# Second half's sum of squares from rows of x, memory's factors behind the first query pair, and no split of x on GpSimd, in the opening of a one-layer hybrid decoder kernel

## The chip, the cores and the metric

One core of one Trainium2 chip runs the kernel. Its five engines are TensorE (PE, with its weight loads as PEld), VectorE (DVE), ScalarE (ACT), GpSimd (POOL) and SyncE (SP, which issues nearly all transfers here). Each takes its own list of instructions in order, and semaphores join them. The metric is the device time of one execution in microseconds; the median of three runs of the kernel before is 894.69 us.

## The reference

One layer over 1024 rows of width 1024, with four cross-attention heads over a memory of 256 rows, four GLA heads and four HGRN2 heads, then a final norm. What the change touches is the head of it:

```python
h = x * rsqrt(mean(x * x, -1) + 1e-6) * norm_w            # 1024 rows
proj = h @ w_in                                           # queries, keys, values, gates of all groups
m = mem * rsqrt(mean(mem * mem, -1) + 1e-6) * mem_norm_w  # 256 rows
mk, mv = split(m @ w_mem_kv)
p = softmax(split_heads(xq) @ mk.T * 128 ** -0.5)         # then p @ mv, norms, silu(gate), w_out
```

## The kernel before

**Tiles.** x comes transposed (`xT`): eight column tiles (128 columns of x by 512 rows) for the first half of the rows, `x[0][k]` (tiles `A_96` to `A_103`), and eight for the second, `x[1][k]` (`A_104` to `A_111`). In products, float32 operands are split in a high part (a cast on ACT, L176 for x, L1269 for weights) and a low part (a subtraction, L177 for x, L1270 for weights), and three matmuls (L1500, L1501, L1502) stand for one product of two tiles.

**Products.** Projections use block sums of x. `A12` and `A11` are the first half's tiles 4 to 7 and 0 to 3, `A22` the second half's tiles 4 to 7, `S1` the second half's tiles 0 to 3 plus 4 to 7, and `S2`, `S3`, `S4` further sums and differences of both halves (`more_sums`). The first query pair `q0` (two heads, `pair_direct`) uses A12, A11, S1 and A22, 24 matmuls each. The gate pair of the first group follows (`pair`): A11, S1, S2, A12, S3, S4, A22, 12 matmuls each. Then cross-attention starts with scores (`sc`).

**Norm.** `norm_x(h)` squares the eight column tiles of a half on ACT (L1366, L1369) and adds them up on DVE (L1370). `norm_x_factors` sums over partitions with four matmuls (L224) and forms the factors (L212 to L217: logarithm and exponential on ACT, one Newton step on DVE). `norm_spread` puts them on a diagonal (L232) and spreads them by a matmul with ones (L233). `norm_scale` scales the tiles on DVE (L1382). `first_half` then splits A12, its low parts on POOL, and A11 on DVE. `second_half` forms S1 and A22; the low parts of A22 alternate between POOL and DVE.

**Memory.** `memory` gives the products for the keys (`key`, L1463), those for the values (`val`, L1474, 16 matmuls in four parts, accumulated in the banks `o` and `kv`), `scales` (the memory rows' factors by the same L224, L212 to L217, L232, L233) and `finish` (keys scaled and split).

**Order.** `run` emits the units in the order of its text. The tile framework then puts each engine's list in an order of its own by data dependences and a model of durations, so that places in the lists move further than the source says. SP takes its transfers in order with eight in flight: each waits for the landing of the one eight places ahead. Weight tiles come by `prefetch` into five buffers `wst`, their parts lie in five buffers each, `whi` and `wlo`.

Of the kernel before, what the change touches and what calls it, by code (L numbers as in the profile page):

```python
# [13 lines left out]
AF = mybir.ActivationFunctionType  # L14
ALU = mybir.AluOpType
AX = mybir.AxisListType
PSUM = bass.MemoryType.PSUM

P = 128
# [5 lines left out]
HALF = S // 2  # L25
# [1193 lines left out]
class Fast(Trunk):  # L1219
# [141 lines left out]
    def norm_x(self, h):  # L1361
# [8 lines left out]
                nc.vector.tensor_tensor(sm, sm, sq, op=ALU.add)  # L1370
        self.sm = sm

    def halves(self, name, x, eng):
        hi, lo = self.a_tile(), self.a_tile()
        self.split((hi, lo), x, eng)
        self.A.setdefault(name, []).append((hi, lo))
# [13 lines left out]
    def first_half(self):  # L1390

        nc = self.nc
        self.A = {}
        self.norm_spread()
        self.norm_scale(0, range(4, 8))
        for k in range(4, 8):
            self.halves("A12", self.x[0][k], nc.gpsimd)
        self.norm_scale(0, range(4))
        for k in range(4):
            self.halves("A11", self.x[0][k], nc.vector)  # L1400

    def second_half(self):

        nc = self.nc
        x, y = self.x
        self.norm_spread()
        self.norm_scale(1, range(4, 8))
        self.norm_scale(1, range(4))
        for k in range(4):
            t = self.t("h", [P, HALF], bufs=2)  # L1410
            nc.vector.tensor_tensor(t, y[k], y[k + 4], op=ALU.add)
            self.halves("S1", t, nc.vector)
            self.halves("A22", y[k + 4], nc.vector if k % 2 else nc.gpsimd)
            nc.vector.tensor_tensor(y[k + 4], t, x[k], op=ALU.subtract)

    def more_sums(self):
# [14 lines left out]
    def memory(self):  # L1431


        nc = self.nc
        mm = nc.tensor.matmul
        scaled = [self.t("mh", [P, 2, M], bufs=4) for _ in range(4)]
        x_ = lambda k: self.memT[k // 4][:, k % 4]
        xs = lambda k: scaled[k // 2][:, k % 2]
        sm = self.t("acc", [P, M], bufs=3)
        rb = self.t("o", [P, M], bufs=self.o_bufs)  # L1440
        col = self.c("col", [P, 8])
        for k in range(KT):
            nc.vector.tensor_scalar(xs(k), x_(k), self.vec[:, V_MNW + k : V_MNW + k + 1], None, op0=ALU.mult)
        for k in range(KT):
            if k == 0:
                nc.scalar.square(sm, x_(k))
            else:
                sq = self.t("h", [P, M], bufs=2)
                nc.scalar.square(sq, x_(k))
                nc.vector.tensor_tensor(sm, sm, sq, op=ALU.add)  # L1450

        self.mk = self.t("v", [P, 2, 4, M], F32R, bufs=1)
        self.mv = self.t("aux", [P, 2, HALF], bufs=1)
        accs, held = [], []

        def key(i):
            def f():
                if i % 2 == 0:
                    held.append(self.ps("tr" if i else "oT", [P, 2, M]))
                ps = held[i // 2][:, i % 2]  # L1460
                for k in range(KT):
                    w = self.mw["mk", i, k // 4][:, (k % 4) * P : (k % 4 + 1) * P]
                    mm(ps, w, xs(k), start=k == 0, stop=k == KT - 1)  # L1463

            return f

        def val(i):
            def f():
                if not accs:
                    accs.extend([self.ps(t, [P, HALF]) for t in ("o", "kv")])  # L1470
                for j in range(2):
                    k = 2 * i + j
                    for b in range(2):
                        mm(accs[b], xs(k)[:, b * P : (b + 1) * P], self.mw["mv", i, j], start=k == 0, stop=k == KT - 1)  # L1474
                if i == 3:
                    for b in range(2):
                        nc.scalar.activation(self.mv[:, b], accs[b], AF.Copy, scale=col[:, b : b + 1])

            return f

        def scales():
            ps = self.ps("sc", [P, M])
            self.factors(sm, col, 2)
            self.spread(ps, col, 2)
            nc.scalar.activation(rb, ps, AF.Copy, scale=QSCALE)

        def finish(j):
            def f():
                t = self.t("h", [P, M], bufs=2)
                nc.vector.tensor_tensor(t, held[j // 2][:, j % 2], rb, op=ALU.mult)  # L1490
                self.split((self.mk[:, 0, j], self.mk[:, 1, j]), t, nc.vector)

            return f

        return [key(i) for i in range(4)], [val(i) for i in range(4)], scales, [finish(j) for j in range(4)]


# [603 lines left out]
    def run(self):  # L2101
        nc = self.nc
        self.scm_i = 0
        self.sums = {}
        groups = [{"kind": kind, "n": n} for kind, n in GROUPS]
        groups[-1]["last"] = True
        first, fill = [], []
        x0, x1 = groups[:2]
        q0 = self.xq_units(x0, 0, self.pair_direct)
        first.append(self.gate_units(x0))  # L2110
        fill.append(self.xq_units(x1, 1) + self.gate_units(x1))
        first.append([])
        for i, g in enumerate(groups):
            if i >= 1:
                if i >= 2:
                    n, kind = g["n"], g["kind"]
                    if kind == "G":
                        u = self.glr_units() if n == 0 else []
                        u += self.gates_gla(g, n) + self.v_units(g, GV + 256 * n)
                        u += self.gate_units(g) + self.qk_units(g, n)  # L2120
                    else:
                        u = self.hf_units(g, n) + self.v_units(g, HI + 256 * n)
                        u += self.gate_units(g) + self.hq_units(g, n)
                    first.append(u)
                fill.append(self.out_units(groups[i - 1], False))
        last = self.out_units(groups[-1], True)

        self.setup()
        key, val, scales, finish = self.memory()
        self.load_x(0, range(8))  # L2130
        self.mw_mv("mv", 0, 1)
        self.load_x(1, range(8))
        self.mw_mv("mv", 2, 3)
        self.prefetch()
        for f in key:
            f()
        self.norm_x(0)
        self.norm_x_factors()
        val[0]()
        self.first_half()  # L2140
        val[1]()
        scales()
        self.norm_x(1)
        self.norm_x_factors()
        val[2]()
        val[3]()
        self.second_half()
        for n, f in enumerate(q0):
            f()
            if n == 7:  # L2150
                self.more_sums()
        for f in finish:
            f()
        for i, g in enumerate(groups):
            self.emit(g, first[i])
            while self.bg or i != 1 and self.tail:
                self.background()
            self.loop(g, fill[i])
        for i, f in enumerate(last):
            f()  # L2160
            if self.tail and (i == 0 or i >= 6):
                self.tail.pop(0)()
        assert self.gcol == NFLAG and self.n_prep == len(self.ops), (self.gcol, self.n_prep, len(self.ops))
# [79 lines left out]
```

## Time and profile before

| | |
|---|---|
| median of 3 runs | 894.69 us (894.6 to 895.03) |
| the profiled execution | 894.56 us, its span 892.8 us |
| PE busy | 856.5 us (96%) |
| DVE, ACT, POOL busy | 626.2, 529.6, 92.5 us |
| PE waits from 20 to 60, 60 to 80, 80 to 100, 100 to 130 us | 4.7, 3.7, 1.9, 0 us |
| granted clock of PE, 43 to 49 us | 0.50 |

The profile's times run from the start of the span; the execution's own time is 1.76 us longer than the span. An engine's row in a timeline has the start, the busy time of the row (several instructions where it ends in x2 and so on), what was done, and in brackets how long the engine sat idle before it and what it waited for. Matmuls overlap, so the pitch of their starts is what one costs. For DVE and ACT too, the pitch is a little below the duration. [...]

### The profile page before, as it was taken

To read this page: it belongs to the slowest core of one execution; us is meant where nothing else is said; L and a number is where in the kernel's file an instruction comes from. 1 tells how busy PE (TensorE), PEld (TensorE's weight loads), DVE (VectorE), ACT (ScalarE), POOL (GpSimd) and SP (SyncE) were. 2 spreads that over 40 slices of the span, in tenths; PEclk is the share of its full clock that TensorE was granted. 3 is DMA by queue.
4 is the path that set the end of the run, shared out by engine and by line. 5 is a ranking of instruction groups with operands and counts; after the bars stand their busy time and mean duration, and the time that the engine had idled before them with its cause. 6 is when DMAs were issued, how large, how long until landed. Compare 5 with 4: busy or idle time off the path is not lost.

```text
span 892.8 us, 13855 instructions
## 1 busy us (share of the span) xinstructions
PE 856.5 (96%) x4742; PEld 714.4 (80%) x4742; DVE 626.2 (70%) x1504; ACT 529.6 (59%) x1273; POOL 92.5 (10%) x111
## 2 busy tenths in 40 slices
PE   8788999999999999999999999999999999999994
PEld 7466887788888898888888898878977878877873
DVE  5879663657648885788648875787685777666676
ACT  4536967987435764467436754466963358942374
POOL 0212112321000110011000110011000011000012
PEclk9989999999999999999999999999999999999997
DMA  9410222451225612472235511473113561034764
GB/s 321 163 48 0 62 69 63 162 199 41 78 84 189 213 49 66 134 236 87 79 107 189 190 60 59 153 229 103 48 48 122 176 208 38 25 110 135 265 220 183
DMA packets 61120, 111.84 MB, mean 125 GB/s; under 512 B 6960, under 2 KB 7088, under 8 KB 61040
## 3 DMA queue, kind: packets, MB, share of 16 engines
q1 hardware_dynamic: 60752, 110.59, 37.4%
q8 instruction: 39, 0.64, 0.3%
q14 instruction: 41, 0.34, 0.1%
q10 hardware_dynamic: 288, 0.28, 0.1%
HBM read 77.28 MB, written 33.55 MB: 124 GB/s over the span
## 4 chain that ended last, share of the span: by engine, by line
PE 69%; DVE 13%; DMA 7%; ACT 7%; issue 3%; SPq 0%; POOL 0%; DVEq 0%; POOLq 0%; ACTq 0%
PE pp L1502 16%; PE pp L1500 16%; PE pp L1501 16%; DMA acc<-sum 3%; DVE acc L1997 2%; PE sc L1500 1%; PE o L1500 1%; DVE A L177 1%; PE sc L1502 1%; DMA A<-w_dram 1%; PE sc L1501 1%; DMA A<-xT_dram 1%; PE oT L982 1%; PE o L1501 1%; PE o L1502 1%
## 5 line engine op out<-in xcount | busy, mean ns | idle before, releaser
L1269 ACT CAST whi<-wst 128x512 fp32r<-128x512 f32 x193 | 117.5, 619 | 181.2 <-PE pp L1501 125.5
L1500 PE MATMUL pp<-A,whi 128*128 128x512 f32 x508 | 203.5, 402 | 3.1 <-ACT A L176 1.5
L1501 PE MATMUL pp<-A,whi 128*128 128x512 f32 x508 | 202.0, 398 | 2.2 <-DVE A L177 2.2
L1502 PE MATMUL pp<-A,wlo 128*128 128x512 f32 x508 | 201.9, 398 | 1.5 <-DVE wlo L1270 1.4
L1270 DVE TENSOR_TENSOR wlo<-wst,whi 128x512 fp32r<-128x512 f32 x193 | 131.7, 689 | 80.9 <-ACT whi L1269 76.3
L1500 PEld LDWEIGHTS pp<-A,whi 128*128 128x128 f32 x508 | 95.8, 189 | 27.5 <-ACT A L176 2.7
L1502 PEld LDWEIGHTS pp<-A,wlo 128*128 128x128 f32 x508 | 95.7, 188 | 26.4 <-DVE wlo L1270 3.6
L1501 PEld LDWEIGHTS pp<-A,whi 128*128 128x128 f32 x508 | 96.0, 189 | 25.6 <-DVE A L177 3.5
L1500 PE MATMUL pp<-whi,mh 128*128 128x512 f32 (+1 forms) x258 | 104.7, 406 | 0.3 <-DVE acc L1997 0.3
L1501 PE MATMUL pp<-wlo,mh 128*128 128x512 f32 (+1 forms) x258 | 102.7, 398 | 0.0
L1502 PE MATMUL pp<-whi,ml 128*128 128x512 f32 (+1 forms) x258 | 101.9, 395 | 0.6 <-POOL ml L992 0.6
L1997 DVE TENSOR_TENSOR acc<-acc,pp 128x512 f32<-128x512 f32 x112 | 76.6, 685 | 31.9 <-PE pp L1502 14.5
L992 POOL TENSOR_TENSOR ml<-h,mh 128x512 fp32r<-128x512 f32 x30 | 41.1, 1369 | 334.4 <-ACT mh L990 334.3
L1262 DVE TENSOR_TENSOR wst<-wst 128x512 f32<-128x512 f32 x82 | 56.9, 694 | 1.5
L1502 PEld LDWEIGHTS pp<-whi,ml 128*128 128x128 f32 x258 | 48.7, 189 | 10.4 <-POOL ml L992 1.0
L1501 PEld LDWEIGHTS pp<-wlo,mh 128*128 128x128 f32 x258 | 48.8, 189 | 7.8 <-DVE wlo L1270 0.3
L1500 PEld LDWEIGHTS pp<-whi,mh 128*128 128x128 f32 x258 | 48.7, 189 | 7.9 <-DVE acc L1997 0.5
L177 POOL TENSOR_TENSOR qk<-qk 128x128 fp32r<-128x128 f32 x28 | 13.0, 470 | 292.8 <-ACT qk L176 253.6
L1955 ACT ACTIVATE o<-o,rs_r 128x128 f32<-128x128 f32 (+1 forms) x96 | 34.2, 427 | 8.7 <-DVE rs_r L195 6.9
L1949 ACT ACTIVATE junk<-o 128x128 bf16<-128x128 f32 (+1 forms) x96 | 32.7, 342 | 1.1
L1946 ACT COPY o<-o 128x256 f32<-128x256 f32 x64 | 23.6, 369 | 15.7 <-PE o L1918 4.7
L990 ACT CAST mh<-h 128x512 fp32r<-128x512 f32 x32 | 19.8, 618 | 21.2 <-DVE h L987 21.1
(278 smaller groups left out, 1860.9 us busy)
## 6 DMA issues: line engine op xcount, KB each, us to landing
wst<-w_dram SPq DMA_DIRECT2D x128, 256.0 KB, 2.6
sum<-acc SPq DMA_DIRECT2D x112, 256.0 KB, 2.1
acc<-sum SPq DMA_DIRECT2D x96, 256.0 KB, 2.8
A<-w_dram SPq DMA_DIRECT2D x16, 256.0 KB, 5.4
A<-xT_dram SPq DMA_DIRECT2D x16, 256.0 KB, 5.4
acc<-x_dram SPq DMA_DIRECT2D x16, 256.0 KB, 2.9
A<-sum SPq DMA_DIRECT2D x16, 256.0 KB, 4.0
out_dram<-A SPq DMA_DIRECT2D x15, 256.0 KB, 2.1
```

The costliest lines, as they stand in the source:

```text
L177: eng.tensor_tensor(to[1], x, to[0].bitcast(F32), op=ALU.subtract)
L992: eng.tensor_tensor(lo, x, hi.bitcast(F32), op=ALU.subtract)
L1262: nc.vector.tensor_tensor(d, a, b, op=ALU.subtract)
L1269: nc.scalar.copy(hi, x)
L1270: nc.vector.tensor_tensor(lo, x, hi.bitcast(F32), op=ALU.subtract)
L1500: mm(out, lhs[0], rhs[0], start=first, stop=False, skip_group_check=skip)
L1501: mm(out, lhs[0], rhs[1], start=False, stop=False, skip_group_check=skip)
L1502: mm(out, lhs[1], rhs[0], start=False, stop=last, skip_group_check=skip)
L1946: nc.scalar.copy(osb, o)
L1949: nc.scalar.activation(junk[:, s * w : (s + 1) * w], osb[:, s], AF.Square, accum_out=g["ss"][:, c % 4, s : s + 1])
L1955: self.nc.scalar.activation(x, x, AF.Copy, scale=r)
L1997: nc.vector.tensor_tensor(dst, dst, ps, op=ALU.add)
```

## The change

It does six things, all in the head of the kernel:

- The four parts of the value weights are loaded right behind the first half's columns, then the first five query weight tiles (`prefetch`), then eight tiles of x by rows (`load_rows`: rows 512 to 1023, two tiles of 128 rows by 512 columns for each block of 128 rows), and then only the second half's columns.
- The second half's sum of squares comes from these row tiles: eight squares on ACT with its accumulator, one reduction on DVE, and the factors by `rsqrt_act` straight from them (`rows_factors`). The call of `norm_x(1)` with its eight squares and seven sums, and the four matmuls of its `norm_x_factors`, go.
- All value products stand before the first query pair.
- `second_half` is emitted after the fourth unit of the first query pair (behind its A12 products).
- `scales`, with the copies of the values that need its factors, is emitted behind the first query pair.
- The low parts of A12 (four) and of A22 (the two that POOL had) are formed on DVE.

```diff
+    def load_rows(self):
+        self.rows = []
+        for b in range(4):
+            for d in range(2):
+                t = self.t("ml" if d else "sg", [P, HALF], bufs=4)
+                self.nc.sync.dma_start(t, self.a["x"][:, 4 + b, d * HALF : (d + 1) * HALF])
+                self.rows.append(t)
+
+    def rows_factors(self):
+        nc = self.nc
+        ss = self.t("fss", [P, 4, 2])
+        for i, t in enumerate(self.rows):
+            nc.scalar.activation(t, t, AF.Square, accum_out=ss[:, i // 2, i % 2 : i % 2 + 1])
+        self.col = self.t("rs_r", [P, 8])
+        t = self.t("rs_t", [P, 8])
+        nc.vector.tensor_reduce(t[:, :4], ss, axis=AX.X, op=ALU.add)
+        self.rsqrt_act(self.col[:, :4], t[:, :4], t[:, 4:8])
...
         for k in range(4, 8):
-            self.halves("A12", self.x[0][k], nc.gpsimd)
+            self.halves("A12", self.x[0][k], nc.vector)
...
-            self.halves("A22", y[k + 4], nc.vector if k % 2 else nc.gpsimd)
+            self.halves("A22", y[k + 4], nc.vector)
...
-                if i == 3:
-                    for b in range(2):
-                        nc.scalar.activation(self.mv[:, b], accs[b], AF.Copy, scale=col[:, b : b + 1])
...
             nc.scalar.activation(rb, ps, AF.Copy, scale=QSCALE)
+            for b in range(2):
+                nc.scalar.activation(self.mv[:, b], accs[b], AF.Copy, scale=col[:, b : b + 1])
...
         self.load_x(0, range(8))
-        self.mw_mv("mv", 0, 1)
+        self.mw_mv("mv", 0, 1, 2, 3)
+        self.prefetch()
+        self.load_rows()
         self.load_x(1, range(8))
-        self.mw_mv("mv", 2, 3)
-        self.prefetch()
...
         self.first_half()
-        val[1]()
-        scales()
-        self.norm_x(1)
-        self.norm_x_factors()
-        val[2]()
-        val[3]()
-        self.second_half()
+        for f in val[1:]:
+            f()
+        self.rows_factors()
         for n, f in enumerate(q0):
             f()
+            if n == 3:
+                self.second_half()
             if n == 7:
                 self.more_sums()
+        scales()
```

The order of the lists moves at three places. The first is ACT, from the square of the first half's first column tile on. `A_96` to `A_103` are the first half's columns, `acc` its running sum, `sg` a square; before:

```order
L1366 ACTIVATE acc_273<-A_96 128x512
L1369 ACTIVATE sg_275<-A_97 128x512
L1369 ACTIVATE sg_278<-A_98 128x512
L1369 ACTIVATE sg_281<-A_99 128x512
L1369 ACTIVATE sg_284<-A_100 128x512
L1369 ACTIVATE sg_287<-A_101 128x512
L1369 ACTIVATE sg_290<-A_102 128x512
L1369 ACTIVATE sg_293<-A_103 128x512
L212 ACTIVATE rs_r_296<-pp_297,eps_73 128x4
```

The same place now, with query weights `wst_221` to `wst_227` and row tiles `sg_231`, `ml_233`, `sg_235`, `ml_237` among them (L1386 is the square with the accumulator):

```order
L1366 ACTIVATE acc_289<-A_96 128x512
L1269 CAST whi_408<-wst_223 128x512
L1269 CAST whi_412<-wst_227 128x512
L1269 CAST whi_416<-wst_221 128x512
L1269 CAST whi_433<-wst_225 128x512
L1269 CAST whi_509<-wst_223 128x512
L1386 ACTIVATE sg_231,fss_389<-sg_231 128x512
L1386 ACTIVATE ml_233,fss_389<-ml_233 128x512
L1386 ACTIVATE sg_235,fss_389<-sg_235 128x512
L1369 ACTIVATE sg_291<-A_97 128x512
L1369 ACTIVATE sg_294<-A_98 128x512
L1386 ACTIVATE ml_237,fss_389<-ml_237 128x512
```

Five casts of query weights and five squares of row tiles moved in between the first and the last square of the first half (the square of A_103 follows the fifth row tile's), and the last three row tiles stand between that square and the factors' L212.

The second is DVE, around the scaling of the second half's first tile `A_108` (L1401 is the scaling now). Before, the eight scalings of the first half, its low parts and those of the query weights had all been done by then:

```order
L1270 TENSOR_TENSOR wlo_528<-wst_231,whi_527 128x512
L232 TENSOR_SCALAR h_426<-ident_69,rs_r_403 128x128 x4
L1270 TENSOR_TENSOR wlo_552<-wst_235,whi_551 128x512
L1270 TENSOR_TENSOR wlo_656<-wst_237,whi_655 128x512
L1382 SCALAR_TENSOR_TENSOR A_108<-A_108,vec_71,sc_425 128x512
L1382 SCALAR_TENSOR_TENSOR A_109<-A_109,vec_71,sc_425 128x512
L1382 SCALAR_TENSOR_TENSOR A_110<-A_110,vec_71,sc_425 128x512
```

The same place now; `A_354` is the last low part of A12, `A_362` to `A_374` are those of A11:

```order
L177 TENSOR_TENSOR A_354<-A_103,A_353 128x512
L1401 SCALAR_TENSOR_TENSOR A_99<-A_99,vec_71,sc_330 128x512
L177 TENSOR_TENSOR A_362<-A_96,A_361 128x512
L1270 TENSOR_TENSOR wlo_534<-wst_227,whi_533 128x512
L177 TENSOR_TENSOR A_366<-A_97,A_365 128x512
L1401 SCALAR_TENSOR_TENSOR A_108<-A_108,vec_71,sc_449 128x512
L177 TENSOR_TENSOR A_370<-A_98,A_369 128x512
L1401 SCALAR_TENSOR_TENSOR A_109<-A_109,vec_71,sc_449 128x512
L177 TENSOR_TENSOR A_374<-A_99,A_373 128x512
L1401 SCALAR_TENSOR_TENSOR A_110<-A_110,vec_71,sc_449 128x512
```

All low parts of the first half moved in line behind its scalings on DVE, the last two of them between scalings of the second half.

The third is PE, where the S1 products of the query pair begin (`pp_629` and `pp_642`, high part `A_442`, low part `A_443`). Before, the gate pair's A11 products (`pp_706`, weights `whi_655`) stand among them:

```order
L1500 MATMUL pp_629<-A_442,whi_493 128x512
L1500 MATMUL pp_642<-A_442,whi_510 128x512
L1500 MATMUL pp_706<-A_345,whi_655 128x512
L1501 MATMUL pp_706<-A_346,whi_655 128x512
L1502 MATMUL pp_706<-A_345,wlo_656 128x512
L1500 MATMUL pp_706<-A_349,whi_655 128x512
L1501 MATMUL pp_629<-A_443,whi_493 128x512
L1502 MATMUL pp_629<-A_442,wlo_494 128x512
L1500 MATMUL pp_629<-A_453,whi_493 128x512
L1501 MATMUL pp_642<-A_443,whi_510 128x512
L1502 MATMUL pp_642<-A_442,wlo_511 128x512
L1500 MATMUL pp_642<-A_453,whi_510 128x512
```

The same place now (`pp_611`, `pp_624`, high parts `A_466`, `A_477`, low parts `A_467`, `A_478`; L224 sums the memory rows' squares):

```order
L1518 MATMUL pp_611<-A_466,whi_416 128x512
L1518 MATMUL pp_624<-A_466,whi_433 128x512
L224 MATMUL pp_673<-ones_70,acc_170 128x1 x2
L1519 MATMUL pp_611<-A_467,whi_416 128x512
L1520 MATMUL pp_611<-A_466,wlo_417 128x512
L1519 MATMUL pp_624<-A_467,whi_433 128x512
L1520 MATMUL pp_624<-A_466,wlo_434 128x512
L1518 MATMUL pp_611<-A_477,whi_416 128x512
L1518 MATMUL pp_624<-A_477,whi_433 128x512
L1519 MATMUL pp_611<-A_478,whi_416 128x512
L1520 MATMUL pp_611<-A_477,wlo_417 128x512
```

The gate pair's A11 products moved out of the S1 stretch to behind A22 of the query pair, and memory's two sums moved in. From the first score blocks on, the lists of the two kernels are the same but for a few swaps of neighbours.

## Rows read from the trace of the kernel before

**Rows 1.** The page's first part: busy time, share of the span and number of instructions of each engine.

```profile
PE 856.5 (96%) x4742; PEld 714.4 (80%) x4742; DVE 626.2 (70%) x1504; ACT 529.6 (59%) x1273; POOL 92.5 (10%) x111
```

**Rows 2.** Who waited for whom, PE alone, from 20 to 60 us, from 60 to 80 us and from 80 to 100 us (two rows each): us in total, times, longest us.

```profile
PE sc L233 <- DVE h L232: 3.5, 1, 3.5
PE pp L224 <- DVE acc L1370: 1.2, 1, 1.2
...
PE pp L1501 <- DVE A L177: 2.2, 3, 1.0
PE pp L1500 <- ACT A L176: 1.5, 1, 1.5
...
PE sc L1501 <- DVE v L177: 1.3, 1, 1.3
PE pp L1502 <- DVE wlo L1270: 0.6, 1, 0.6
```

**Rows 3.** Stretches of the span, PE alone: stretch, its length, PE busy (instructions), granted clock, busy share of the DMA engines, GB/s.

```profile
42.00:43.00 1.00, 0.19 (x1) 0.66 0.00 0
43.00:46.00 3.00, 3.00 (x12) 0.50 0.00 0
46.00:49.00 3.00, 3.00 (x9) 0.50 0.28 87
49.00:50.00 1.00, 1.00 (x6) 0.93 0.77 260
...
60.00:72.00 12.00, 9.28 (x35) 1.00 0.01 1
```

**Rows 4.** PE's timeline, two neighbours in the first stretch at low clock and two behind it.

```profile
46.79 0.63 PE L1501 MATMUL pp<-A,whi 128*128 128x512 f32 x1
47.21 0.63 PE L1502 MATMUL pp<-A,wlo 128*128 128x512 f32 x1
...
50.19 0.40 PE L1500 MATMUL pp<-A,whi 128*128 128x512 f32 x1
50.43 0.39 PE L1501 MATMUL pp<-A,whi 128*128 128x512 f32 x1
```

**Rows 5.** PE's timeline, the last matmul of the gate pair's A22 product, and two of the first scores (six such stand in one block).

```profile
97.98 0.39 PE L1502 MATMUL pp<-A,wlo 128*128 128x512 f32 x1
...
99.94 0.28 PE L1501 MATMUL sc<-v,wup 128*128 128x256 f32 x1
100.06 0.28 PE L1502 MATMUL sc<-v,wup 128*128 128x256 f32 x1
```

**Rows 6.** SP's timeline, the first issue of a column tile of the first half and, twelve transfers later, that of the second half; then, from the answer on this line, the time from issue to landing.

```profile
8.72 0.33 SPq L1296 DMA_DIRECT2D A<-xT_dram  x1
...
16.83 0.33 SPq L1296 DMA_DIRECT2D A<-xT_dram  x1
...
DMA to landing us min/median/max: 5.4/5.4/6.0
```

**Rows 7.** ACT's timeline: the first square of the first half, five squares in a row, four casts in a row, and a square with its accumulator followed by the next.

```profile
14.13 0.63 ACT L1366 ACTIVATE acc<-A 128x512 f32<-128x512 f32 x1 [2.18 <-DMA A<-xT_dram]
...
24.10 2.83 ACT L1369 ACTIVATE sg<-A 128x512 f32<-128x512 f32 x5
...
30.89 2.16 ACT L176 CAST A<-A 128x512 fp32r<-128x512 f32 x4
...
106.60 0.31 ACT L1949 ACTIVATE junk<-o 128x128 bf16<-128x128 f32 x1
106.81 0.19 ACT L1949 ACTIVATION_READ_ACCUMULATOR junk<-o 128x1 f32 x1
106.91 0.30 ACT L1949 ACTIVATE junk<-o 128x128 bf16<-128x128 f32 x1
```

**Rows 8.** The first half's factors, in the timelines of PE (first and last value product, the four sums and the product behind them), of ACT and of DVE.

```profile
21.33 1.02 PE L1474 MATMUL o<-A,mh 128*128 128x512 f32 x2
22.19 0.95 PE L224 MATMUL pp<-ones,acc 128*128 128x1 f32 x8
23.00 1.10 PE L1474 MATMUL kv<-A,mh 128*128 128x512 f32 x2
...
36.40 1.02 PE L1474 MATMUL kv<-A,mh 128*128 128x512 f32 x2
...
23.17 0.26 ACT L212 ACTIVATE rs_r<-pp,eps 128x4 f32<-128x4 f32 x1 [3.61 <-PE pp L224]
...
26.71 5.36 DVE L1382 SCALAR_TENSOR_TENSOR A<-A,vec,sc 128x512 f32<-128x512 f32 x8 [0.74 <-PE sc L233]
```

**Rows 9.** DVE's timeline: the scaling of the second half and what follows, and the wait for POOL.

```profile
53.52 5.35 DVE L1382 SCALAR_TENSOR_TENSOR A<-A,vec,sc 128x512 f32<-128x512 f32 x8
58.78 1.29 DVE L1411 TENSOR_TENSOR h<-A 128x512 f32<-128x512 f32 x2
59.99 0.68 DVE L1425 TENSOR_TENSOR A<-A 128x512 f32<-128x512 f32 x1
...
63.48 0.69 DVE L1414 TENSOR_TENSOR A<-h,A 128x512 f32<-128x512 f32 x1 [1.60 <-POOL A L177]
```

**Rows 10.** PE's timeline: the spread of the second half's factors behind the A12 products, and the last wait of the S1 stretch.

```profile
52.29 1.02 PE L233 MATMUL sc<-h,ones 128*128 128x512 f32 x2
...
71.34 0.51 PE L1501 MATMUL pp<-A,whi 128*128 128x512 f32 x1 [0.41 <-DVE A L177]
```

## The prediction

> **What bounds the kernel now.** The page's busy shares come first: PE is busy 856.5 of 892.8 us [rows 1], so the change, which takes next to nothing from PE, can only act through time in which PE waits or runs at half clock. The list of PE's waits says where: 4.7 us between 20 and 60 us, 3.7 between 60 and 80, 1.9 between 80 and 100 [rows 2]. The windows with the granted clock add a second loss: it falls in the microsecond from 42, stands at 0.50, and comes back in the one from 49 [rows 3]. A matmul of 128x512 then starts every 0.43 us and not every 0.235 [rows 4]. Behind the gate pair's last product, which ends its pitch at 97.98 + 0.23 = 98.2 [rows 5], PE's order is nearly that of before and dense, so I measure the change at this point, and carry the difference to the end one for one.
>
> **The change, part by part: transfers.** Twelve issues took 16.83 - 8.72 = 8.1 us, 0.676 each, and each landed 5.4 later [rows 6]. So transfer n, counted from the first half's first column, lands at 14.1 + 0.676n. In the new queue the first half keeps 0 to 7; the value weights take 8 to 15, the query weights 16 to 20, the row tiles 21 to 28, the second half's columns 29 to 36. The second query weight lands at 25.6, the fourth at 27.0, the last row tile at 33.0, the last column at 38.5. The row tiles have the size and the row length of the columns, so I give them the same pace.
>
> **The change: ACT, and the first half's factors.** Removed are eight squares of columns, added eight of rows with the accumulator. That is no saving on the path, because of where they stand. ACT squares the first column at 14.13 as before [rows 7], and then meets the casts of query weights, the first of which waits for 25.6, the second for 27.0. It goes on in line: four casts at 0.52 (2.16 less the last one's 0.61, over three) end at 29.1. Up to the square of the first half's last column stand five row squares and six plain ones. Plain: 0.55, from five in 2.83. With the accumulator I take 0.65: the narrow ones follow each other at their full 0.31, where plain ones gain some 0.1 on their duration [rows 7]. That is 5 x 0.65 + 6 x 0.55 = 6.55, so the last square starts at 35.6 and ends at 36.2. One more sum (0.69) and four small matmuls (23.00 - 22.19 = 0.81) give 37.7, but three more row squares hold ACT to 38.2 before it reaches the factors' logarithm. Before, that stood at 23.17, and the first scaled tile at 26.71, 3.54 later [rows 8]; with some 0.2 for the second chain of factors woven in, the first scaling starts at **41.9**. The first half's scaling is thus 15.2 us later than before.
>
> **The change: value products, idle PE, the clock.** All 16 value products now run at once, from 21.33 at a pitch of 0.86 [rows 8]: they end at 35.1. Nothing is left to fill the wait for the factors. The first four scalings take 4 x 0.67 (5.36 over 8), the first low part 0.69: dense work starts at 45.3, where it started at 44.5 before. From 35.1 to 45.3 PE has about 2.5 us to do (sums, spread, two matmuls). Before, a wait of 3.5 us and one of 1.2 were enough for the low clock, and 6.3 us lay between the first dense work at 42.8 and the full clock [rows 2, 3]. I take it to fall again. Of A12's 24 matmuls 22 are left at 45.3. If the clock came back at 49.1, as before, nine would run at 0.43 and thirteen at 0.235, to 52.2; if 6.3 us after 45.3, to 53.3. I take the middle, **52.7**; it was 52.3. DVE's low parts, 1.27 apart with a scaling between (the last at 49.1), don't bind in this case.
>
> **The change: the second half.** Its factors are now ready long before they are used; the six low parts that DVE takes over cost 6 x 0.60, its seven sums of squares free 7 x 0.60. But the scaling stands in DVE's line behind a query weight's low part, whose cast needs a buffer that PE frees two matmuls before the end of A12: 52.2 + 0.6 + 0.6, and one more low part give 54.1. The spread asks for less: its consumer ran 53.52 - 52.29 = 1.23 behind it, which is 53.9 here [rows 9, 10]. Eight scalings and two low parts (8 x 0.67 + 2 x 0.6) end at **60.7**, against 58.9 before. From there to the last low part of S1 stand 19 operations of 0.60 [rows 9]: 72.2, and four matmuls later, at 73.2, S1 is through. Before, PE went on from the last low part at 71.34 and S1 was through four matmuls later, at 72.4 [rows 10], though DVE had waited 1.6 us for POOL's split on the way [rows 9]. The wait for POOL does go; it is spent on the later start.
>
> **The change: what filled the waits.** By 72.4 PE had also done the gate pair's twelve A11 products (2.8 us) inside the waits of the S1 stretch; now they come behind A22. That is the largest term of the loss. From 73.2: A22 24 x 0.235 = 5.6; the gate pair's A11 and S1 the same 5.6; memory's spread, which before ended the wait of 3.5 us [rows 2] in idle time, 0.5 (half of the wider one's 1.02 [rows 10]): 84.9. Then S2 waits for a low part 25.7 us of DVE's list behind 60.7, at 86.4, and for the first scores, whose operand ACT hands over at about 86.7, since memory's factors come late. Ten more matmuls, four products of twelve and five score matmuls of 0.12 [rows 5] give 86.9 + 2.3 + 11.2 + 0.6 = **101.0**. Before, the waits of 1.3 and 0.6 us in this part [rows 2] were on the path; they are replaced by this one. The sum: 101.0 - 98.2 = +2.8 us. Against the profiled execution's 894.56, that is 897.4; the median, 894.69, is 0.1 above that execution, so the two hardly differ.
>
> **The rivals.** (1) *The clock falls a second time.* Between the end of A11 (the last low part at 56.7, nine matmuls, 58.8) and the first high part of S1 (61.9) PE has 3 us without work, and then works 1.4 of each 3.0 us, since the fillers are gone. Before, the stretch from 60 to 72 had 9.28 us busy of 12 and kept its clock [rows 3]; a wait of 3.5 us, though, came ahead of the fall at 42. If it falls, DVE's pace hides the slow matmuls up to the last four (+0.8), and some 5.5 us of half clock behind them cost 2.7; a part goes into the wait for S2: +5.3 in all, 899.9. [...] The trace has one fall behind one longer wait, and none in the shorter waits of 60 to 72.
>
> (2) *The clock holds at 42* (not slower). Then DVE's low parts pace A12, to 50.1, the second half is scaled by 58.1, S2 resumes at 84.3, and the point lies at 98.4: +0.2, 894.8. For it: PE does get some work every few microseconds. Against it: less than before the fall in the trace. It decides if the clock still stands at 1.00 at 45.
>
> (3) *The factors come earlier, at a full clock* (faster). If casts and squares ran closer than their pitches here, so that the first scaling starts at 40.0 instead of 41.9, everything behind it moves up by 1.9: 892.9. Price and point: the case is faster only from a start below 40.3, with the clock held.
>
> (4) *It does not do what it says*, that is, the lists read above don't bind as they stand. Each engine takes its list in order in the trace, so this has little chance.
>
> **How the numbers follow.** A measurement of this kernel can tell about 0.2%, 1.8 us, from no change. The sum holds with 0.48 (895.6 to 898.8, by the bounds of the clock's return, 0.5 each way, and of about thirty pitches); a fifth of that lies within 1.8 us. Rival 1: 0.25. Rival 2: 0.17, nearly all within 1.8. Rival 3: 0.08, faster. Rival 4: 0.02. Slower: 0.38 + 0.25 = 0.63; same: 0.10 + 0.15 + 0.02 = 0.27; faster: 0.10. The forecast is 897.4. The range takes rival 2 with some room below and rival 1 with a microsecond above: 893.6 to 900.9.
>
> **What the profile would show.** Right: ACT idle from 14.8 to about 25.6 behind its first square; the value products without a gap to 35.1; the first scaling near 41.9; a granted clock of 0.50 at 45; the second half's scaling done near 60.7; waits of PE for DVE's low parts between 59 and 72 of 6 us and more; a wait of PE near 86. Wrong: a first scaling before 40, a clock of 1.00 at 45, or an end of the gate pair before 98. The forecast fails low if the row tiles land earlier than counted, and high if S1's waits take the clock down.

## The result, and the profile after

The changed kernel takes 901.03 us (median; 900.5 to 902.88) where the kernel before takes 894.86 beside it (894.6 to 895.26): the ratio is 1.0072, 95% interval 1.0055 to 1.009, so it is 6.2 us slower, and the interval goes from 4.9 to 8.1. The forecast was 897.4, 2.8 us slower, with a range up to 900.9. Its profiled execution took 900.64 us, with a span of 898.9.

The page's busy line first, in the form of [rows 1]. PE has 4 us more of busy time, and eight matmul records fewer:

```profile
PE 860.7 (96%) x4734; PEld 716.1 (80%) x4734; DVE 623.8 (69%) x1504; ACT 525.1 (58%) x1277; POOL 78.8 (9%) x105
```

Then the head, in the order of the prediction. ACT's timeline answers to [rows 7]: the first casts of query weights, and the last squares of the first half's columns.

```profile
25.79 0.62 ACT L1269 CAST whi<-wst 128x512 fp32r<-128x512 f32 x1 [11.29 <-DMA wst<-w_dram]
27.04 2.18 ACT L1269 CAST whi<-wst 128x512 fp32r<-128x512 f32 x4 [0.63 <-DMA wst<-w_dram]
...
34.29 1.65 ACT L1369 ACTIVATE sg<-A 128x512 f32<-128x512 f32 x3
```

ACT is idle for 11.3 us behind its first square, as forecast, and the first half's last square ends at 35.9. DVE's timeline answers to [rows 8, 9]: the first scaling, the last six scalings of the second half, and what follows.

```profile
42.84 2.72 DVE L1401 SCALAR_TENSOR_TENSOR A<-A,vec,sc 128x512 f32<-128x512 f32 x4 [1.19 <-PE sc L233]
...
56.62 4.03 DVE L1401 SCALAR_TENSOR_TENSOR A<-A,vec,sc 128x512 f32<-128x512 f32 x6
60.57 1.43 DVE L1430 TENSOR_TENSOR h<-A 128x512 f32<-128x512 f32 x2
```

PE alone by stretches, columns as in [rows 3]:

```profile
40.00:48.00 8.00, 5.08 (x8) 0.50 0.00 0
48.00:50.00 2.00, 2.00 (x8) 0.74 0.00 0
...
62.00:64.00 2.00, 1.89 (x8) 0.67 0.00 0
64.00:66.00 2.00, 2.00 (x6) 0.50 0.00 0
66.00:68.00 2.00, 1.93 (x7) 0.97 0.00 0
```

The clock is down at 40 already and back at 49, and it is down a second time between 62 and 66. PE's waits, as in [rows 2]: four rows from 20 to 60 us, two from 60 to 80, one from 80 to 110.

```profile
PE sc L233 <- DVE h L232: 2.4, 1, 2.4
PE pp L224 <- DVE acc L1370: 2.3, 1, 2.3
PE pp L1518 <- ACT A L176: 1.5, 1, 1.5
PE pp L1519 <- DVE A L177: 0.7, 1, 0.7
...
PE pp L1518 <- ACT A L176: 2.7, 1, 2.7
PE pp L1519 <- DVE A L177: 2.1, 2, 1.0
...
PE sc L1518 <- ACT v L176: 0.9, 1, 0.9
```

PE's timeline: the spread of the first half's factors (at half clock, against [rows 10] at full clock), the first score, the gate pair's last matmul, the first and the last of five scores behind it ([rows 5]), and three matmuls of the body.

```profile
40.73 2.08 PE L233 MATMUL sc<-h,ones 128*128 128x512 f32 x2 [2.40 <-DVE h L232]
...
86.57 0.38 PE L1518 MATMUL sc<-v,wup 128*128 128x256 f32 x1 [0.94 <-ACT v L176]
...
100.14 0.40 PE L1520 MATMUL pp<-A,wlo 128*128 128x512 f32 x1
100.38 0.28 PE L1519 MATMUL sc<-v,wup 128*128 128x256 f32 x1
...
100.83 0.28 PE L1520 MATMUL sc<-v,wup 128*128 128x256 f32 x1
...
120.16 0.39 PE L1519 MATMUL pp<-A,whi 128*128 128x512 f32 x1
...
315.68 0.33 PE L982 MATMUL oT<-ident,o 128*128 128x128 f32 x1 [2.10 <-ACT o L1973]
...
860.36 0.49 PE L1934 MATMUL o<-v,scm 128*128 128x128 f32 x2 [1.16 <-ACT o L1964]
```

The fifth score ends its pitch of 0.12 at 100.95: the forecast for this point was 101.0. The same three matmuls of the body in the kernel before, PE's timeline of the profiled execution:

```profile
117.32 0.48 PE L1501 MATMUL pp<-A,whi 128*128 128x512 f32 x1
...
310.25 0.33 PE L982 MATMUL oT<-ident,o 128*128 128x128 f32 x1 [0.59 <-ACT o L1955]
...
853.69 0.49 PE L1916 MATMUL o<-v,scm 128*128 128x128 f32 x2 [0.73 <-ACT o L1946]
```

Here stands the surprise. The shift is 120.16 - 117.32 = 2.84 us behind the head, where 2.8 was forecast, but 5.43 at the second matmul and 6.67 at the third, though PE's order between them hardly differs. Between these marks the shift also creeps, by some 0.25 us in every 50 to 100 us, where PE waits for nothing. So two questions were left for the experiments: what the body adds to 2.8, and whether the head is late for the reason that the prediction gave.

### The profile page after: what moved, and what is told of

Same layout as the page of the kernel before. It is cut to its first block, busy times and chain, and to the rows that moved or that the text cites. A ratio compares the mean times of both kernels' runs of the same rounds, so it can differ in the third digit from the quotient of the medians.

```text
span 898.9 us, 13836 instructions
## 1 busy us (share of the span) xinstructions
PE 860.7 (96%) x4734; PEld 716.1 (80%) x4734; DVE 623.8 (69%) x1504; ACT 525.1 (58%) x1277; POOL 78.8 (9%) x105
## 4 chain that ended last, share of the span: by engine, by line
PE 69%; DVE 12%; ACT 9%; DMA 8%; issue 3%; SPq 0%; DVEq 0%; ACTq 0%
PE pp L1519 16%; PE pp L1520 16%; PE pp L1518 16%; DMA acc<-sum 2%; ACT L1753 2%; DVE acc L2015 2%; DMA sum<-acc 2%; PE o L1518 1%; DMA A<-w_dram 1%; PE oT L982 1%; PE sc L1518 1%; DVE wlo L1270 1%; PE o L1520 1%; PE o L1519 1%; DMA acc<-x_dram 1%
## 5 line engine op out<-in xcount | busy, mean ns | idle before, releaser
L1519 PE MATMUL pp<-wlo,mh 128*128 128x512 f32 (+1 forms) x258 | 102.9, 399 | 0.0
L1520 PE MATMUL pp<-whi,ml 128*128 128x512 f32 (+1 forms) x258 | 102.1, 396 | 0.6 <-POOL ml L992 0.6
```

The source lines that it names most:

```text
L1519: mm(out, lhs[0], rhs[1], start=False, stop=False, skip_group_check=skip)
L1520: mm(out, lhs[1], rhs[0], start=False, stop=last, skip_group_check=skip)
```

## The experiments

The runs were made in three groups. Each group has a chip of its own, on which the kernel before ran too, so kernels are compared by their ratio to it.

**The kernel before, again** (no edit).

> The kernel before, unchanged, run again beside the others. If the 3.3 us that the changed kernel loses behind the gate pair are its own, this runs at 894.5 to 895.5 us and its dense matmuls of 128x512 keep the mean pitch of 232.9 ns that the profile before has (the profile after has 233.8). If those 3.3 us are only a difference between executions or chips, this comes out as far from 894.7, 1.5 us or more, or its pitch is 233.5 or more.

896.05 us, ratio 1.0007 (0.999 to 1.0024). Single executions on this chip spread more, from 891.7 to 897.9 us in 29 runs of the kernel before. PE's timeline, the same three matmuls:

```profile
117.35 0.48 PE L1501 MATMUL pp<-A,whi 128*128 128x512 f32 x1
...
312.57 0.33 PE L982 MATMUL oT<-ident,o 128*128 128x128 f32 x1 [2.09 <-ACT o L1955]
...
856.30 0.49 PE L1916 MATMUL o<-v,scm 128*128 128x128 f32 x2 [1.42 <-ACT o L1946]
```

Against the first execution of the same kernel the shift is 0.03 in the head, 2.3 at the second mark, 1.5 of it from the wait there (2.09 us and not 0.59), and 2.6 at the third. This wait comes and goes with the execution; in the profile after, the chain to it holds a load of a stored sum that took 5.3 us. Set against this repeat, the kernel after is 2.81, 3.11 and 4.06 us later at the three marks, so its body adds 1.3 us and not 3.8: two single executions cannot tell what the body adds. The pitch, however, is the change's. Taking the distance from one matmul's start to the next one's (pairs 225 to 245 ns apart, behind 130 us; 843 to 852 such pairs in each of the traces of the table below), dense products of x with high weights follow each other every 233.3 ns in both executions of the kernel before, and every 234.2 ns in the kernel after. The granted clock is 1.00 from 130 to 880 us in all of these traces.

**A later head** (28 matmul records that nothing needs, 128x128 each).

```diff
         for f in finish:
             f()
+        gap = self.ps("sc", [P, HALF])
+        for _ in range(14):
+            nc.tensor.matmul(gap[:, :P], self.ones, self.ones, start=True, stop=True)
```

> The kernel before, with 14 matmuls of 128x128 that nothing needs put into PE's line behind the first query pair; nothing else is moved. Estimate from the rows: 14 x 0.06 to 0.2 us, so 1 to 3 us on PE there. Theory A, the body answers to a later head with more waits of its own (PE's clock and the waits for the scores' square and for the last attention tile depend on when it starts): the end comes later by about twice what the gate pair's end does. Theory B, a later head is carried one for one, and the 3.3 us of the changed kernel have another origin: the end comes later by what the gate pair's end does, within 0.7 us. Which of the two is read from the shift of the same matmuls at 100, 300 and 850 us.

895.3 us, ratio 0.9992 (0.9979 to 1.0006). The scheduler dealt the extra matmuls out among PE's waits from 59 to 67 us, and the shift at 95 us was 0.5. So the head was hardly delayed, and the run tells nothing on either theory. It does show that 4.0 us of extra work in those waits costs the kernel nothing that can be told.

**The weights' places in SBUF.** The programs of the two kernels differ in one thing that no order shows: buffers are laid out in the order in which the code first asks for them. `load_rows` asks for `ml` ahead of the weights' halves, so `whi` begins at byte 199104 of a partition, and began at 190784 before. Two kernels give the kernel before other places and change nothing else (in their traces the lists of PE, DVE, ACT and GpSimd are those of the kernel before), by asking for buffers without using them: the places of the kernel after, and a move of 128 bytes (`whi` at 190912).

```diff
+    def norm_x_factors(self):
+        if not hasattr(self, "col"):
+            self.t("ml", [P, HALF], bufs=4)
+        super().norm_x_factors()
+        self.t("fss", [P, 4, 2])
+        self.t("rs_t", [P, 8])
```

> The kernel before with the same instructions in the same order on every engine; only the places of its buffers in SBUF are moved to those of the kernel after (ml ahead of whi, so that whi begins at byte 199104 of a partition and not at 190784). Theory A, what the changed kernel loses behind the gate pair is mostly a longer pitch of dense matmuls that follows from where the weights' halves lie: pitch 233.8 ns where the kernel before has 232.6 to 233.0, and an end 2 to 3 us later, 897 to 898.5 us. Theory B, the pitch belongs to something else in the changed program (its length, where its instructions lie) or the loss is waits alone: pitch 232.9, time as before.

The second leaves out the two lines on `ml`.

> The kernel before, same instructions and order, with whi, wlo and what follows moved by 128 bytes only (whi at 190912). If the pitch follows the offset of the weights' halves within 256 or 512 bytes, it is that of the kernel after, 233.8 ns and 2 to 3 us; if it follows which part of SBUF they lie in, 232.9 ns and the time of before.

The third gives the kernel after the old places of `whi`, `wlo` and `sg`.

```diff
     def load_rows(self):
+        self.t("sg", [P, HALF], bufs=self.sg_bufs)
+        self.t("rs_r", [P, 8])
+        self.t("whi", [P, HALF], F32R, bufs=NSLOT)
+        self.t("wlo", [P, HALF], F32R, bufs=NSLOT)
```

> The kernel after, same instructions and order, with whi and wlo (and sg) put back at the addresses that they have in the kernel before; ml follows them. Theory A: pitch 232.6 to 233.0 ns, the gate pair's end as in the kernel after (101.0) and the end 2 to 3 us earlier than it: 898 to 899 us, near the 897.4 forecast. Theory B: 900.5 to 902.5.

Moved to the places of the kernel after, the kernel before takes 898.03 us, ratio 1.0034 (1.0017 to 1.005), or 3.0 us more; moved by 128 bytes, 897.19, ratio 1.0016 (1.0004 to 1.0028). The kernel after with the old places takes 900.04, ratio 1.0035 (1.0019 to 1.0052). The groups of instructions between 130 and 880 us show it directly; the last number ahead of the idle time is the mean duration in ns. First the kernel before (again), then the same with the places of the kernel after:

```profile
L1501 PE MATMUL pp<-A,whi 128*128 128x512 f32 x416 | 164.6, 396 | 0.0
L1500 PE MATMUL sc<-whi,A 128*128 128x256 f32 x96 | 27.7, 288 | 0.0
```

```profile
L1508 PE MATMUL pp<-A,whi 128*128 128x512 f32 x416 | 165.2, 397 | 0.0
L1507 PE MATMUL sc<-whi,A 128*128 128x256 f32 x96 | 27.9, 291 | 0.0
```

The kernel after, and the kernel after with the old places:

```profile
L1519 PE MATMUL pp<-A,whi 128*128 128x512 f32 x419 | 166.4, 397 | 0.0
L1518 PE MATMUL sc<-whi,A 128*128 128x256 f32 x96 | 27.9, 291 | 0.0
```

```profile
L1522 PE MATMUL pp<-A,whi 128*128 128x512 f32 x421 | 166.6, 396 | 0.0
L1521 PE MATMUL sc<-whi,A 128*128 128x256 f32 x96 | 27.7, 288 | 0.0
```

The durations go with the places and not with the program. The mean distances between starts, worked out from the traces as above, in ns. A distance counts for the product that it starts from, so the three columns of the gates are best read as a sum: 694.9, 700.0, 696.2, 699.9 and 695.5 from top to bottom.

| kernel | `whi` begins at | A,whi | whi,ml | wlo,mh | whi,mh |
|---|---|---|---|---|---|
| before | 190784 | 233.3 | 231.5 | 231.4 | 232.0 |
| before, places of after | 199104 | 234.2 | 233.2 | 233.3 | 233.5 |
| before, moved by 128 bytes | 190912 | 234.2 | 231.4 | 229.8 | 235.0 |
| after | 199104 | 234.2 | 233.2 | 233.2 | 233.5 |
| after, old places of `whi`, `wlo` | 190784 | 233.3 | 231.0 | 233.4 | 231.0 |

One nanosecond counts here: between 130 and 880 us stand 3 x 416 products of x (0.9 ns each, 1.1 us), 3 x 254 of the gates (1.7 ns, 1.3 us) and 1152 narrow ones of 128x256 with the weights' halves (1.7 ns, 1.9 us: their mean distance is 118.3 ns with `whi` at 190784 and 120.0 in the three kernels that have it elsewhere), 4.3 us in all by the count. The swap of places measured 3.0 (1.5 to 4.5) at the end; PE's waits in the body, which differ by 2 us between two executions of the kernel before, can hide the rest. Theory A holds. Which rule of the address makes the pitch stays open: a move by 128 bytes does all of it for the products of x and the narrow ones, but only a quarter for the gates' (1.3 of 5.1 ns). Putting the weights back gave the kernel after some 3 us (1.0072 to 1.0035); its gate pair ended a microsecond later in that execution (102.1), in which the clock came back only at 52.

**The first half's squares in buffers of their own.**

```diff
-                sq = self.t("sg", [P, HALF], bufs=self.sg_bufs)
+                sq = self.t("h", [P, HALF], bufs=2)
                 nc.scalar.square(sq, self.x[h][k])
```

> The kernel after, with one thing changed: the squares of the first half's columns are written to another set of buffers (two of tag h) and no longer to the four of tag sg, in which the row tiles wait to be squared. Theory A, the first half's factors are late (first scaling at 42.84 us) because their squares wait for buffers that row tiles hold: the squares run first, the first scaling starts at about 27 us, the first query product at about 38 without a fall of the granted clock behind it, the second half is scaled by 47, and the gate pair ends at about 87 instead of 101: 883 us, up to 886 if the body adds to it. Theory B, the factors are late because ACT must do casts and row squares by its list whatever the buffers are, or POOL's absence and the late factors of memory set the time: 897 to 901 us.

893.9 us, ratio 0.9985 (0.997 to 1.0). DVE's timeline, the scaling of the first half, and the last two scalings of the second:

```profile
26.26 5.36 DVE L1401 SCALAR_TENSOR_TENSOR A<-A,vec,sc 128x512 f32<-128x512 f32 x8 [1.34 <-PE sc L233]
...
48.38 1.40 DVE L1401 SCALAR_TENSOR_TENSOR A<-A,vec,sc 128x512 f32<-128x512 f32 x2
```

PE alone by stretches:

```profile
40.00:48.00 8.00, 8.00 (x33) 1.00 0.00 0
48.00:60.00 12.00, 9.76 (x40) 1.00 0.06 22
```

The first scaling starts at 26.3 and not at 42.8, PE is dense from 40 us, and no fall of the clock is left. So the first half's factors are late in the kernel after because their squares wait for `sg` buffers, all four of which `load_rows` has taken for tiles that must first land and be squared. Theory A holds in its mechanism. In its size it does not: 883 was expected. The shift against the kernel before is -6.9 us at 117 us, not -11: DVE now paces PE behind 54 us, where three waits for its low parts take 3.0 us; what the rest of the 4 us is was not followed up. The body then takes some 5 of it back in the profiled execution. This kernel still has the new places (234.2 ns for the products of x), by the count above some 4 us, and the wait that comes and goes is 1.5 longer here than in the kernel before (2.05 and 0.59).

**Both edits together.**

> The kernel after with both edits: the first half's squares in buffers of their own (tag h), and whi and wlo at the addresses of the kernel before. Theory A: the 7 us that the first edit gains at 117 us stay 4 to 7 us at the end, 889 to 891.5 us, faster than both kernels. Theory B: as with the first edit alone, 893 to 894.5 us.

890.06 us, ratio 0.9927 (0.9906 to 0.9947): 6.5 us faster than the kernel before, and by the ratios 1.4% below the kernel after. It is the best version here. The places are worth 0.6% in it, some 5 us, and 3.0 in the kernel before; the two were measured on different chips, and why they differ is not known.

**The splits back on GpSimd,** in the kernel after and then in the best version.

```diff
-            self.halves("A12", self.x[0][k], nc.vector)
+            self.halves("A12", self.x[0][k], nc.gpsimd)
...
-            self.halves("A22", y[k + 4], nc.vector)
+            self.halves("A22", y[k + 4], nc.vector if k % 2 else nc.gpsimd)
```

> The kernel after, with the splits of A12 and two of A22 given back to GpSimd, as before the change. Theory A, by the sum of the prediction: what the changed kernel loses is in the order of its head and the lost fillers, and the splits on VectorE are worth at most what VectorE waited for GpSimd (1.6 us) against six low parts of 0.60 us: 899.5 to 902 us. Theory B, the splits on VectorE are what costs, since VectorE paces the S1 stretch: 896 to 898 us, the gate pair's end at 97 to 98.

> The kernel with the first half's squares in their own buffers and the weights' places of before (890.06 us), with the splits of A12 and two of A22 given back to GpSimd. VectorE paces its S1 stretch (PE waits 3.0 us for its low parts), so taking six low parts of 0.6 us off it gains up to 3 us there if GpSimd delivers in time: 887 to 889; if GpSimd is late, as with the kernel after, 890 to 893.

In the kernel after: 902.1 us, ratio 1.0062 (1.0038 to 1.0086), no difference to 1.0072 that can be told. In the best version: 894.66, ratio 1.0006 (0.9992 to 1.0021), 0.8% above the version without the splits, some 7 us, where 3 at the worst were expected; 5.8 of them are there at 117 us already (shift against the kernel before -0.1, and -5.9 without). POOL's and DVE's timelines there show how:

```profile
38.25 4.93 POOL L177 TENSOR_TENSOR A<-A 128x512 fp32r<-128x512 f32 x4 [36.52 <-DVE rs_t L216]
...
39.58 3.89 DVE L232 TENSOR_SCALAR h<-ident,rs_r 128x128 f32<-128x128 f32 x4
...
45.63 2.07 DVE L1404 SCALAR_TENSOR_TENSOR A<-A,vec,sc 128x512 f32<-128x512 f32 x3 [2.17 <-PE sc L233]
```

PE's wait for these diagonals, then DVE's timeline and PE's wait in the best version, with the splits on DVE:

```profile
PE sc L233 <- DVE h L232: 7.2, 1, 7.2
```

```profile
38.51 0.87 DVE L232 TENSOR_SCALAR h<-ident,rs_r 128x128 f32<-128x128 f32 x4
...
40.69 0.75 DVE L1404 SCALAR_TENSOR_TENSOR A<-A,vec,sc 128x512 f32<-128x512 f32 x1
...
PE sc L233 <- DVE h L232: 3.1, 1, 3.1
```

Beside POOL's splits the four diagonals of the spread take 3.89 us and not 0.87, and PE waits 7.2 us for them and not 3.1. Not all of DVE's work was slowed like this: the first half's eight scalings, whose second tensor lies in PSUM, took 5.36 us (43.01 to 48.37) with the splits back in the kernel after, and 5.36 with the splits on DVE (the row at 26.26 above). Most of the former lay beside POOL's splits by an estimate from rows: the first scaling is done at some 43.7, a cast of its tile takes 0.54 [rows 7], and four splits some 5 us (4.93 above), to 49. Whether the splits on DVE gain depends on what DVE has to do at that moment: 6 us where the second half's spread falls beside them, nothing measurable in the kernel after.

**The kernel after, again, and memory's factors back ahead of the first query pair,** the latter in the kernel after and in the best version.

```diff
         self.rows_factors()
+        scales()
         for n, f in enumerate(q0):
...
-        scales()
         for f in finish:
```

> The kernel after, unchanged, beside the others: the measure of how it stands to the kernel before on this chip (first seen 1.0072), and to the kernels below. If the split of the loss is right (2.8 us in the head, 2 to 3 in the pitch, the rest in waits that come and go), the gate pair ends again at 101.0 and the pitch is 233.8 to 234.0 ns; the wait for the attention tile near 316 us may be there or not.

> The kernel after, with memory's factors put back ahead of the first query pair. Theory A, they matter little: VectorE's order lets S2 go on at 86.4 and the late factors only to 86.7, so the end is within 1 us of the kernel after. Theory B, the late factors set the restart of PE at 86.6 and push the scores behind it: 2 us or more earlier than the kernel after. Theory C, put back, they delay the casts of the first half: 1 to 2 us later.

> The same kernel (890.06 us), with memory's factors put back ahead of the first query pair instead. If their late place matters little: 889 to 891; if it costs what the fillers are worth, 887 to 888.5.

The kernel after again: 900.94 us, ratio 1.0077 (1.0056 to 1.0098), the first of its gate pair's last five scores 0.34 us later than in its first profile, the pitch 234.25. With memory's factors put back: 900.47, ratio 1.008 (1.0054 to 1.0106), so their place costs nothing that can be told. In the best version: 891.17, ratio 0.996 (0.9944 to 0.9977), no gain either, and if anything a loss.

## Why the prediction went wrong

**The head was right, in part by luck.** Forecast and trace: second query weight's cast 25.6 and 25.79, first scaling 41.9 and 42.84, the spread behind A12 52.7 and 52.74, end of the second half's scaling 60.7 and 60.65, first score 86.7 and 86.57, gate pair with its scores 101.0 and 100.95. The clock fell as forecast, and the difference behind the head is 2.84 us where 2.8 was summed, 3.2 in the second profile of the kernel after. Two misses cancel in it: the first scaling came 0.9 late, because the spread ahead of it ran at half clock (2.08 us for the two matmuls, 1.02 at full clock), which the sum had left out; and the clock was back at 49.0, the early bound of the two whose middle the sum took. PE waited 4.8 us between 60 and 80, of which 2.1 for DVE's low parts, where 6 and more for these were given as a sign; matmuls at half clock filled part of that time. That the lost fillers are the largest term of the head stays argued: no run put them back.

**The step that failed is "carry the difference to the end one for one".** It rested on PE's order, which is nearly that of before. The order says nothing on places, and the places make the dense matmuls 0.9 to 1.7 ns longer: 3.0 us (1.5 to 4.5) measured by moving the buffers alone. The sum had this term at nothing. With the head's 2.8 that is 5.8 of the 6.2 measured (4.9 to 8.1). What is left lies within the intervals; the wait at 310 to 316 us, which makes the profiled executions differ by 1.5 us more, is no part of it, since the kernel before has it too in another execution.

**The reason given for the late factors was incomplete.** The prediction read ACT's order as it stands and priced it rightly, but took the order for the cause. It is the scheduler's answer to the four `sg` buffers. As the price was read from the order, the sum did not suffer; a forecast of what another version could gain would have.

**The rivals.** Rival 1's second fall of the clock did come, at 62 to 66 us, and its time, 899.9, is nearest to the result, but for the wrong reason: the stretch through S1 ended at 73.3 where 73.2 was forecast without the fall, because the clock was back at 66 and DVE's pace hid the slow matmuls until then. Where it stayed down longer there was a cost: in the profiled execution of the kernel after with the splits on GpSimd, the slowest of its six, the clock came back only at 74.9, and the gate pair ended at 102.9, though the splits may have a part in that. In the profile after, a fall followed the wait of 2.7 us and none the waits of 1.0 and 0.9 us behind it, and the fall cost nothing. Rivals 2 to 4 did not occur. That the wait for POOL "does go" but "is spent on the later start" fits the run with the splits back: there DVE waits 1.6 us for POOL again, and the time is the same.

## What to carry to other kernels

Ahead of a change that adds a buffer or asks for one earlier, compare the addresses of the large operands, not only the order of instructions: in a kernel that is 96% dense matmuls, a nanosecond of pitch is 0.4% of its time, by an estimate from the pitch (1 of 233). When an order looks bad, ask which buffer it waits for before moving work; here one line on a buffer's tag, and four on places, made the same change 1.4% faster than as written, some 13 us. An addition to the end is only as sure as the stretch it is carried through, so a range must hold something for that stretch too.

## What the runs showed of the hardware

- The pitch of a dense matmul depended on where its operands lie in SBUF, at the same granted clock of 1.00: 233.3 or 234.2 ns for the 128x512 products of x, 118.3 or 120.0 for the narrow ones of 128x256. A move by 128 bytes was enough.
- One and the same kernel waited 0.59 us in one execution and 2.09 in another for the same attention tile, and its executions on one chip spread over 6 us.
- Four DVE operations of 128x128 with one tensor input took 3.89 us beside GpSimd's splits, and 0.87 without. Eight of 128x512 with one of their two tensors in PSUM took 5.36 us, most of it beside such splits by the estimate above, and 5.36 without.
